# First attention: the softmax of seven of eight head pairs normalised after the product with the values

## The chip, the cores and the metric

The kernel runs on one core of one Trainium2 chip. The metric is the device time of one execution in microseconds (us). A measured time is the median of several runs; the profile comes from one further execution.

## What is computed

Two transformer layers over 512 tokens of 1024 features, in float32, each with adaptive scale and shift, a mixer, and a squared-ReLU MLP. Layer 0 uses a sparse attention with 16 heads (eight pairs), layer 1 a differential attention. The change is in layer 0, whose core is this (`mask` stands for the 128 chosen keys and for the relative bias):

```
def block(args):
    ...
    logits = jnp.einsum('bqhr,bqkr->bhqk', q_lat, kv_sel).astype(jnp.float32)
    bias = rel_bias[_rel_bucket(tpos[None, :, None] - sel)]
    logits = logits + jnp.transpose(bias, (0, 3, 1, 2))
    logits = jnp.where(valid[:, None], logits, NEG)
    p = jax.nn.softmax(logits, axis=-1).astype(h.dtype)
    o_lat = jnp.einsum('bhqk,bqkr->bqhr', p, kv_sel)
    return jnp.einsum('bhqr,hrd->bqhd', o_lat, w_uv)
...
return o.reshape(B, S, A_HEADS * A_V_DIM) @ w_o
```

The softmax divides each row of exponentials by its sum. Whether that division is done on the exponentials or on the product with the values, the result is the same.

## The kernel before, in words

The tokens lie in four tiles of 128 (`i` = 0 to 3), the heads in pairs `p` = 0 to 7 with `m` = 0, 1. One item of the first attention is (p, i, m): a 128-row tile of queries of one head against its 128(i+1) causal keys, so the four tiles are 128, 256, 384 and 512 wide. A function `attend` runs over the 64 items in order. For item n it issues the scores, and for item n - 4 the product with the values:

- `score`: two matmuls into a PSUM bank "l" (L646, L647), a VectorE (DVE) pass that adds mask and bias and finds the row's extreme (L670, L673; the mask with bias comes from GpSimd, L662 and L666), and ScalarE (ACT) exponentials into a tile `ex`, whose row sums go to one of eight columns of the pair's `sums` (L679).
- `pv_a` (the product): reciprocal of the row sum (L943), scaling of the exponentials by it (L944), both on DVE; then `transposed`: TensorE (PE) transposes of the i+1 blocks into a PSUM bank "t" (L687) and a copy to the tile `pt`, by ACT for m = 0 (L690) and by DVE for m = 1 (L692); and, once m = 1 is there, the products of both heads into the pair's bank "o" (L954): head m fills rows 64m to 64m+63, columns are queries.
- `done_a`, after a pair's last item: ACT copies bank "o" to a page `vo` (`bm` for the last pair) (L960), from which the output projection takes its operand (split into a high and a low part by L133 and L134).

PSUM has eight banks, two for each of "d", "l", "t" and "o". While a pair runs, `make_a` prepares the one two ahead: the transposed key weights `uk` (L781) into a "t" bank, keys into a "d" bank (L158 to L160), and copies by DMA. The output projection's steps (L984 to L986) begin inside the last pair and go on behind it; its weights are prepared by ACT (L148) and GpSimd (L153) in pairs 2 to 7. DVE also works off modulation steps at the end of the attention (L433, L435), each on a quarter-megabyte half of a weight row that SP loads into one of three `raw` buffers. What follows the attention begins with the residual's additions (L488).

The order of instructions on each engine is not written out by hand: a scheduler with a model of the chip sets it when the program is built, so an edit in `pv_a` moves its neighbours on all engines. Engines execute their own order strictly and wait for each other by semaphores.

Of the kernel before, what the change touches and what calls it, by code (L numbers as in the profile page):

```python
# [15 lines left out]
ALU = mybir.AluOpType  # L16
# [3 lines left out]
P = 128  # L20
# [3 lines left out]
NT = S // P  # L24
DFF = 4096
HEADS = 16
HD = 64
# [40 lines left out]
def hybrid_kernel(  # L68
# [8 lines left out]
    nc = tc.nc  # L77
    x = x[0]
    out = out[0]
# [11 lines left out]
    def nm(s):  # L91
        uid[0] += 1
        return f"{s}_{uid[0]}"
# [3 lines left out]
    def page(dt=F32, tag="pg"):  # L97
        return pg.tile([P, 512], dt, tag=tag, name=nm(tag), bufs=GB[tag])
# [3 lines left out]
    def temp(tag, dt=F32):  # L102
        return tp.tile([P, 512], dt, tag=tag, name=nm(tag), bufs=TB[tag])

    def small(shape, tag, bufs=4):
        return tp.tile(shape, F32, tag=tag, name=nm(tag), bufs=bufs)
# [3 lines left out]
    def bank(tag):  # L110
        return ps.tile([P, 512], F32, tag=tag, name=nm("ps" + tag), bufs=PB[tag])
# [3 lines left out]
    def wide_bank():  # L115

        tag = ("d", "d", "l", "l", "o", "o")[cyc[0] % 6]
        cyc[0] += 1
        return bank(tag)
# [43 lines left out]
    ident = cp.tile([P, P], F32, name="ident")  # L163
# [137 lines left out]
    for d in range(DC // 2):  # L301
# [10 lines left out]
        for j in range(2):  # L312
            kc = 2 * d + j
            a = (hT[0][:, kc, :], hT[1][:, kc, :])
# [306 lines left out]
    def attend(pairs, make, mask, pv, done, out, LA, early=None, depth=1, group=0, side=iter(()),  # L621
# [18 lines left out]
        def score(it):  # L640
            p, i, m = it
            q, (kh, kl) = qk[p][m]
            W = P * (i + 1)
            h = 2 * p + m
            lp = bank("l")
            nc.tensor.matmul(lp[:, 0:W], q[:, P * i : P * (i + 1)], kl[:, 0:W], start=True, stop=False)  # L646
            nc.tensor.matmul(lp[:, 0:W], q[:, P * i : P * (i + 1)], kh[:, 0:W], start=False, stop=True)  # L647
            neg = temp("neg")
# [6 lines left out]
            near = near[:, ::-1]  # L655
            n0 = max(0, W - 256)
            init = 3e38
            if mask is not None and i >= 3:
                if (i, m) not in full:
                    full[i, m] = page()  # L660
                    nc.gpsimd.tensor_copy(full[i, m][:, 0:n0], mask[i][:, 0:n0])
                marks["p"] = nc.gpsimd.tensor_tensor(out=full[i, m][:, n0:W], in0=mask[i][:, n0:W], in1=near, op=ALU.add).ins  # L662
                near, n0 = full[i, m][:, 0:W], 0
            elif mask is not None and i > 0:
# [74 lines left out]
        for _ in ahead:  # L739
# [7 lines left out]
                            op0=ALU.mult)  # L747
# [55 lines left out]
    for i in range(1, NT):  # L803
        W = P * (i + 1)
        acc = page()
        work[i] = acc
        for h in range(IDXH):
# [4 lines left out]
            r = temp("neg")  # L812
# [4 lines left out]
            else:  # L817
                nc.vector.scalar_tensor_tensor(out=acc[:, 0:W], in0=r[:, 0:W], scalar=s, in1=acc[:, 0:W],
                                               op0=ALU.mult, op1=ALU.add)
# [5 lines left out]
    for i in range(NT):  # L825
        if i % 2 == 0:
            ckb.append(bank("t"))
        o = ckb[-1][:, 256 * (i % 2) : 256 * (i % 2) + 256]
        for k in range(DC):
# [11 lines left out]
    rb = cp.tile([BUCKETS, HEADS], F32, name="rb")  # L841
# [8 lines left out]
                            op0=ALU.subtract)  # L850
# [12 lines left out]
                            op=ALU.mult)  # L863
    lsum = small([1, 4], "lsum", 1)
    nc.vector.tensor_reduce(out=lsum[:, 0:2], in_=lpr.rearrange("o (a d) -> o a d", a=2), axis=mybir.AxisListType.X,
                            op=ALU.add)
# [18 lines left out]
    for i in range(NT):  # L885
        nc.vector.tensor_scalar(out=ckn[i // 2][:, 256 * (i % 2) : 256 * (i % 2) + 256], in0=ck_ps[i],
                                scalar1=ckss[:, i : i + 1], scalar2=None, op0=ALU.mult)
# [17 lines left out]
    for h in range(2):  # L905
        for i in range(NT):
            o = bank("d")
# [28 lines left out]
    a_state = {}  # L936
    oA = {}

    def pv_a(p, i, m, es, sums, transposed):
        W = P * (i + 1)  # L940
        e = es[p, i, m]
        r = small([P, 1], "rs")
        nc.vector.reciprocal(r, sums[:, 2 * i + m : 2 * i + m + 1])  # L943
        nc.vector.tensor_scalar(out=e[:, 0:W], in0=e[:, 0:W], scalar1=r, scalar2=None, op0=ALU.mult)  # L944
        t = transposed(e, i, m == 0)
        a_state[p, i, m] = t
        if i == 0 and m == 0:
            a_state["o", p] = bank("o")
        if m == 1:
            o = a_state["o", p]  # L950
            for j in range(i + 1):
                for mm in range(2):
                    h = 2 * p + mm
                    nc.tensor.matmul(o[64 * mm : 64 * mm + 64, P * i : P * (i + 1)],  # L954
                                     V[j][h // 8][:, 64 * (h % 8) : 64 * (h % 8) + 64],
                                     a_state[p, i, mm][:, P * j : P * (j + 1)], start=(j == 0), stop=(j == i))

    def done_a(p):
        oA[p] = temp("bm") if p == 7 else page(tag="vo")
        nc.scalar.copy(oA[p], a_state["o", p])  # L960

    def mixer_out(w, src, R, ln_idx, prepare, mT, ring, order, late=lambda: None):

# [79 lines left out]
    def scale_residual():  # L1043
        for i in range(NT):
            for h in range(2):
                nc.scalar.activation(R[i][h], R[i][h], AF.Copy, scale=ALPHA)

    attend(range(8), make_a, work, pv_a, done_a, mixer_out(a_w_o[0], oA, R, (0, 0), before_out_a, mT, 6, {(2, 1, 3): "lead", (3, 1, 0): 0, (3, 1, 3): 1}, scale_residual), 4, topk, 2, 2, side)


# [76 lines left out]
    for i in range(NT):  # L1127
        o = wide_bank()
# [6 lines left out]
        t = page()  # L1135
# [129 lines left out]
```

## Time and profile before

| | |
|---|---|
| time, median of 3 runs | 1312.59 us (1311.4 to 1314.78) |
| the profiled execution: its own time | 1311.5 us |
| its span, first to last instruction | 1309.7 us |
| PE busy | 1267.0 us (97%) |
| DVE busy | 741.5 us (57%) |
| ACT busy | 504.2 us (38%) |
| GpSimd busy | 570.5 us (44%) |
| mean granted clock of PE | 0.989 |

How to read it: shares are averages over stages with different limits. The first attention's products run from 172 to 296 us. PE's ends are modelled and its instructions overlap, so a busy PE is not always a PE at its peak; PEld is its weight loads, which overlap the matmuls. The trace names an instruction by its line, engine, operation and tiles (output <- inputs, buffer numbers left out). A helper that records many operations gives them all its own line.

### The profile page before, as it was taken

The numbers are of one execution on the slowest core, as the hardware profiler recorded it, in microseconds if no ns is written. First come the engines' busy times: TensorE is split into PE (matmuls) and PEld (weight loads), VectorE is DVE, ScalarE is ACT, GpSimd is POOL, SyncE is SP. The second block draws the span as 40 slices with busy tenths as digits, with TensorE's granted clock in tenths as the row PEclk, the third lists the DMA queues.
The fourth block names the chain that finished last, engine by engine and source line by source line (L and its number), as shares of the span: only waits on it lengthen the run. The fifth ranks groups of instructions, "written<-read, shape, count | busy, mean of one in ns | idle before, by whom it ended". The sixth has DMA issues, their size and how long they took to land.

```text
span 1309.7 us, 17697 instructions
## 1 busy us (share of the span) xinstructions
PE 1267.0 (97%) x6354; PEld 1013.4 (77%) x6354; DVE 741.5 (57%) x1553; ACT 504.2 (38%) x965; POOL 570.5 (44%) x469
## 2 busy tenths in 40 slices
PE   6999999998999999999999999999899999999997
PEld 4775566677988878878788898877798888888885
DVE  2487859968642774764646376684853342332437
ACT  2554247824432422412315555682453232231320
POOL 1614348604486235234134873451539623424403
PEclk9999999999999999999999999999999999999998
DMA  9727577543623684684422633440144333333311
GB/s 308 215 82 223 168 199 200 150 137 104 187 93 108 201 256 118 210 277 141 141 81 65 177 82 104 129 129 1 49 145 125 100 97 97 97 97 97 97 49 64
DMA packets 169135, 176.79 MB, mean 135 GB/s; under 512 B 13564, under 2 KB 121432, under 8 KB 169048
## 3 DMA queue, kind: packets, MB, share of 16 engines
q1 hardware_dynamic: 169048, 175.67, 45.1%
q8 instruction: 50, 0.82, 0.3%
q14 instruction: 37, 0.30, 0.1%
HBM read 160.93 MB, written 2.12 MB: 124 GB/s over the span
## 4 chain that ended last, share of the span: by engine, by line
PE 72%; DVE 6%; POOL 2%; issue 1%; ACT 1%; DMA 0%; POOLq 0%; DVEq 0%
PE psd L158 5%; PE psd L160 5%; PE psd L159 5%; PE psl L158 3%; PE psl L159 3%; PE psl L160 3%; PE psl L578 3%; PE psl L580 3%; PE psl L579 3%; PE pso L580 3%; PE pso L578 3%; PE psd L580 3%; PE pso L579 3%; PE pso L158 3%; PE psd L578 3%; PE pso L159 3%
## 5 line engine op out<-in xcount | busy, mean ns | idle before, releaser
L153 POOL TENSOR_TENSOR wl<-raw,wh 128x512 fp32r<-128x512 f32 (+1 forms) x226 | 302.2, 1361 | 505.5 <-ACT wh L148 477.7
L148 ACT CAST wh<-raw 128x1024 fp32r<-128x1024 f32 x181 | 189.8, 1050 | 425.0 <-PE psd L580 77.9
L153 DVE TENSOR_TENSOR wl<-raw,wh 128x1024 fp32r<-128x1024 f32 x68 | 91.1, 1339 | 150.0 <-ACT wh L148 150.0
L158 PE MATMUL psd<-htl,wh 128*128 128x512 f32 (+1 forms) x400 | 157.0, 392 | 3.2 <-DVE htl L134 2.7
L159 PE MATMUL psd<-hth,wh 128*128 128x512 f32 (+1 forms) x400 | 155.1, 388 | 0.0
L160 PE MATMUL psd<-hth,wl 128*128 128x512 f32 (+1 forms) x400 | 154.7, 387 | 0.0
L489 POOL TENSOR_TENSOR rq<-rq,pt 128x512 f32<-128x512 f32 x66 | 96.7, 1495 | 76.2 <-DVE pt L488 76.1
L158 PEld LDWEIGHTS psd<-htl,wh 128*128 128x128 f32 x400 | 76.6, 191 | 25.9 <-DVE htl L134 6.0
L679 ACT ACTIVATE ex<-neg,mx 128x128 f32<-128x128 f32 (+3 forms) x128 | 72.1, 564 | 50.3 <-DVE mx L673 42.5
L160 PEld LDWEIGHTS psd<-hth,wl 128*128 128x128 f32 x400 | 76.7, 192 | 16.3 <-issue 1.7
L159 PEld LDWEIGHTS psd<-hth,wh 128*128 128x128 f32 x400 | 76.7, 192 | 13.7 <-issue 0.8
L158 PE MATMUL psl<-htl,wh 128*128 128x512 f32 (+1 forms) x224 | 82.2, 367 | 4.2 <-DVE htl L134 4.2
L159 PE MATMUL psl<-hth,wh 128*128 128x512 f32 (+1 forms) x224 | 81.9, 366 | 0.0
L160 PE MATMUL psl<-hth,wl 128*128 128x512 f32 (+1 forms) x224 | 81.3, 364 | 0.0
L134 DVE TENSOR_TENSOR pg<-ex,pg 128x512 fp32r<-128x512 f32 x66 | 60.4, 917 | 27.1 <-ACT pg L133 27.1
L580 PE MATMUL psl<-wh,pg 128*128 128x512 f32 x176 | 68.9, 391 | 0.0
L578 PE MATMUL pso<-wh,pg 128*128 128x512 f32 x176 | 68.8, 391 | 0.0
L580 PE MATMUL pso<-wh,pg 128*128 128x512 f32 x176 | 68.7, 390 | 0.0
L578 PE MATMUL psl<-wh,pg 128*128 128x512 f32 x176 | 68.7, 390 | 0.0
L579 PE MATMUL pso<-wl,pg 128*128 128x512 f32 x176 | 68.7, 390 | 0.0
L579 PE MATMUL psl<-wl,pg 128*128 128x512 f32 x176 | 68.5, 389 | 0.0
L159 PE MATMUL pso<-hth,wh 128*128 128x512 f32 (+2 forms) x184 | 68.3, 371 | 0.0
(311 smaller groups left out, 2920.9 us busy)
## 6 DMA issues: line engine op xcount, KB each, us to landing
raw<-in_mlp_w_dram SPq DMA_DIRECT2D x128, 512.0 KB, 4.1
raw<-in_ada_w_dram SPq DMA_DIRECT2D x32, 512.0 KB, 4.2
hk<-in_ada_w_dram SPq DMA_DIRECT2D x48, 256.0 KB, 3.6
bm<-in_ada_w_dram SPq DMA_DIRECT2D x48, 256.0 KB, 4.9
raw<-in_b_w_in_dram SPq DMA_DIRECT2D x24, 512.0 KB, 4.0
pg<-pg SPq DMA_DIRECT2D x84, 128.0 KB, 2.4
pg<-in_ada_w_dram SPq DMA_DIRECT2D x32, 256.0 KB, 6.0
raw<-in_a_w_in_dram SPq DMA_DIRECT2D x14, 512.0 KB, 5.1
```

The lines of the kernel that those rows point to most:

```text
L134: eng.tensor_tensor(out=L, in0=src, in1=f(H), op=ALU.subtract)
L148: nc.scalar.copy(Hv, r)
L153: eng.tensor_tensor(out=Lv[:, a:b], in0=r[:, a:b], in1=f(Hv[:, a:b]), op=ALU.subtract)
L158: nc.tensor.matmul(o, w[0], a[1], start=first, stop=False)
L159: nc.tensor.matmul(o, w[0], a[0], start=False, stop=False)
L160: nc.tensor.matmul(o, w[1], a[0], start=False, stop=last)
L489: eng.tensor_tensor(out=R[h], in0=R[h], in1=t, op=ALU.add)
L578: nc.tensor.matmul(o, al[1], wr[0], start=(k == 0), stop=False)
L579: nc.tensor.matmul(o, al[0], wr[1], start=False, stop=False)
L580: nc.tensor.matmul(o, al[0], wr[0], start=False, stop=(k == nk - 1))
L679: marks["a"] = nc.scalar.activation(e[:, 0:W], neg[:, 0:W], AF.Exp, bias=mx[:, 0:1], scale=-1.0, accum_out=sums[:, m : m + 1]).ins
```

## The change

For pairs 0 to 6 the exponentials are no longer scaled: they are transposed as they are, and the transposed copies are all made by DVE. At a pair's last tile (i = 3, m = 0) DVE takes the reciprocal of all eight row sums at once, spreads each over 64 columns of a page, PE transposes that page in four blocks of 128 so that queries become columns, and DVE copies the result back to the page. `done_a` then multiplies the pair's product by that page on DVE, in place of ACT's copy. For pair 7 all stays, its m = 0 copies on ACT too.

```diff
     def pv_a(p, i, m, es, sums, transposed):
-        W = P * (i + 1)
-        e = es[p, i, m]
-        r = small([P, 1], "rs")
-        nc.vector.reciprocal(r, sums[:, 2 * i + m : 2 * i + m + 1])
-        nc.vector.tensor_scalar(out=e[:, 0:W], in0=e[:, 0:W], scalar1=r, scalar2=None, op0=ALU.mult)
-        t = transposed(e, i, m == 0)
+        if p == 7:
+
+            r = small([P, 1], "rs")
+            nc.vector.reciprocal(r, sums[:, 2 * i + m : 2 * i + m + 1])
+            e = es[p, i, m][:, 0 : P * (i + 1)]
+            nc.vector.tensor_scalar(out=e, in0=e, scalar1=r, scalar2=None, op0=ALU.mult)
+        elif i == NT - 1 and m == 0:
+
+            r = small([P, 2 * NT], "rs8", 2)
+            nc.vector.reciprocal(r, sums)
+            a_state["r", p] = page()
+            nc.vector.tensor_copy(a_state["r", p].rearrange("q (a d) -> q a d", d=HD),
+                                  r.unsqueeze(2).to_broadcast([P, 2 * NT, HD]))
+            rb = bank("t")
+            for j in range(NT):
+                c = slice(P * j, P * (j + 1))
+                nc.tensor.transpose(rb[:, c], a_state["r", p][:, c], ident)
+            nc.vector.tensor_copy(a_state["r", p], rb)
+        t = transposed(es[p, i, m], i, p == 7 and m == 0)
         a_state[p, i, m] = t
...
     def done_a(p):
         oA[p] = temp("bm") if p == 7 else page(tag="vo")
-        nc.scalar.copy(oA[p], a_state["o", p])
+        if p == 7:
+            nc.scalar.copy(oA[p], a_state["o", p])
+        else:
+            nc.vector.tensor_tensor(out=oA[p], in0=a_state["o", p], in1=a_state["r", p], op=ALU.mult)
```

In the changed file the reciprocal is L949, the broadcast L951, the added transposes L956, their copy L957, the products with the values L967, the scaling of the product L976, pair 7's reciprocal and scaling L943 and L945, and the output projection L1000 to L1002 (L984 to L986 before).

The scheduler's order changes on all engines within the first attention, and nowhere behind it. Three places follow. On DVE, in the middle of the attention (the end of pair 2), before:

```order
L943 RECIPROCAL rs_2235<-sums_1944 128x1
L944 TENSOR_SCALAR ex_2127<-ex_2127,rs_2235 128x512
L673 ISA neg_2190,mx_2191<-psl_2187,hk_1741 128x128
L673 ISA mx_2191 128x1
L943 RECIPROCAL rs_2259<-sums_1944 128x1
L673 ISA neg_2221,mx_2222<-psl_2218,bm_2223 128x256
L673 ISA mx_2222 128x1
L943 RECIPROCAL rs_2300<-sums_2164 128x1
L944 TENSOR_SCALAR ex_2144<-ex_2144,rs_2259 128x512
L692 COPY pt_2210<-pst_2206 128x384
L944 TENSOR_SCALAR ex_2165<-ex_2165,rs_2300 128x128
```

and of the change (`rs_584` holds eight reciprocals, `pg_2191` is the page they are spread over, `pst_2193` its transposed bank, and the `neg` rows evacuate scores of the next pair):

```order
L949 RECIPROCAL rs_584_2189<-sums_1918 128x8
L673 ISA neg_2175,mx_2176<-psl_2172,bm_2177 128x256
L673 ISA mx_2176 128x1
L692 COPY pt_2112<-pst_2109 128x256
L951 COPY pg_2191<-rs_584_2189 128x512
L692 COPY pt_2142<-pst_2138 128x384
L673 ISA neg_2209,mx_2210<-psl_2206,bm_2211 128x256
L673 ISA mx_2210 128x1
L692 COPY pt_2164<-pst_2160 128x384
L670 ISA neg_2240,mx_2241<-psl_2237,pg_594 128x128
```

The scalings are gone, copies of transposed weights stand in their places, and the broadcast comes three DVE steps behind the reciprocal. On PE at the end of the attention, where pair 7's last tile is transposed and multiplied, before (`pst_3328` is the last transposed tile, `pt_3333` its copy by DVE, and L984 to L986 are steps of the output projection):

```order
L687 MATMUL pst_3328<-ident,ex_3277 128x128 x4
L986 MATMUL psl_3503<-wh_2295,pg_3132 128x512
L984 MATMUL psl_3503<-wh_2393,vo_3174 128x512
L985 MATMUL psl_3503<-wl_2394,pg_3173 128x512
L986 MATMUL psl_3503<-wh_2393,pg_3173 128x512
L984 MATMUL psl_3503<-wh_2515,vo_3219 128x512
L985 MATMUL psl_3503<-wl_2516,pg_3218 128x512
L986 MATMUL psl_3503<-wh_2515,pg_3218 128x512
L984 MATMUL psl_3503<-pg_2613,vo_3250 128x512
L985 MATMUL psl_3503<-pg_2615,pg_3249 128x512
L986 MATMUL psl_3503<-pg_2613,pg_3249 128x512
L954 MATMUL pso_3206<-pt_3323,rq_991 64x128
```

and of the change (`pst_3230` is the last transposed tile, `pt_3235` its copy by DVE, `pt_3225` that of the other head by ACT, `pt_3200` and `pt_3209` belong to the tile before):

```order
L1002 MATMUL psl_3405<-pg_2545,pg_3151 128x512
L687 MATMUL pst_3230<-ident,ex_3179 128x128 x4
L967 MATMUL pso_3108<-pt_3209,rq_991 64x128
L967 MATMUL pso_3108<-pt_3200,rq_1000 64x128
L967 MATMUL pso_3108<-pt_3209,rq_1000 64x128
L967 MATMUL pso_3108<-pt_3200,rq_1009 64x128
L967 MATMUL pso_3108<-pt_3209,rq_1009 64x128
L967 MATMUL pso_3108<-pt_3225,rq_991 64x128
L967 MATMUL pso_3108<-pt_3235,rq_991 64x128
```

Ten steps of the projection stood between the last transposes and the products that need their copy; now five products of the tile before stand there. On DVE ahead of the same copy, before:

```order
L692 COPY pt_3307<-pst_3303 128x384
L435 SCALAR_TENSOR_TENSOR pg_3345<-raw_3371,sil,pg_3345 128x512
L435 SCALAR_TENSOR_TENSOR pg_3346<-raw_3371,sil,pg_3346 128x512
L435 SCALAR_TENSOR_TENSOR pg_3345<-raw_3375,sil,pg_3345 128x512
L435 SCALAR_TENSOR_TENSOR pg_3346<-raw_3375,sil,pg_3346 128x512
L692 COPY pt_3333<-pst_3328 128x512
```

and of the change, from pair 6's product to the first modulation steps and their neighbours:

```order
L976 TENSOR_TENSOR vo_3062<-pso_2846,pg_3012 128x512
L134 TENSOR_TENSOR vo_3076<-vo_2650,pg_3075 128x512
L945 TENSOR_SCALAR ex_3179<-ex_3179,rs_3227 128x512
L433 TENSOR_SCALAR pg_3247<-raw_3249,sil 128x512
L433 TENSOR_SCALAR pg_3248<-raw_3249,sil 128x512
L435 SCALAR_TENSOR_TENSOR pg_3247<-raw_3253,sil,pg_3247 128x512
L435 SCALAR_TENSOR_TENSOR pg_3248<-raw_3253,sil,pg_3248 128x512
L134 TENSOR_TENSOR vo_3152<-vo_3062,pg_3151 128x512
L692 COPY pt_3187<-pst_3184 128x256
```

The sixteen modulation steps (two L433, fourteen L435) now start behind pair 6's product on DVE; before, that product was copied by ACT. The copies of pair 7's last two tiles (384 and 512 wide) still stand among and behind them.

## Rows read from the trace of the kernel before

**Rows 1.** Windows of one pair each: us; busy PE, PEld, DVE, ACT, POOL; PE clock; DMA.

```profile
189.90:202.50 12.60, 12.60 (x92) 8.95 (x89) 11.36 (x45) 10.68 (x29) 9.73 (x12) 1.00 0.63 155
202.50:216.20 13.70, 12.63 (x93) 9.06 (x88) 13.45 (x49) 9.42 (x27) 12.61 (x13) 1.00 0.65 178
216.20:229.40 13.20, 11.39 (x85) 8.16 (x84) 12.48 (x43) 10.89 (x30) 10.49 (x12) 1.00 0.80 224
229.40:240.50 11.10, 10.28 (x83) 7.38 (x81) 8.80 (x34) 9.67 (x28) 8.78 (x10) 1.00 0.83 243
240.50:251.30 10.80, 9.88 (x68) 6.67 (x64) 10.31 (x38) 8.01 (x24) 7.12 (x8) 1.00 0.66 148
```

**Rows 2.** Waits, 200 to 250 us: us in total, times, longest.

```profile
PE psl L646 <- DVE mx L673: 2.5, 4, 1.1
```

**Rows 3.** Groups by line, 200 to 250 us, PEld: busy, mean ns, idle before and releasers.

```profile
L954 PEld LDWEIGHTS pso<-pt,rq 128*64 128x64 f32 x160 | 10.6, 136 | 6.1 <-issue 1.3 <-ACT pt L690 1.2 <-DVE pt L692 1.0
L687 PEld LDWEIGHTS pst<-ident,ex 128*128 128x128 f32 x80 | 9.1, 140 | 5.3 <-issue 4.1 <-PE pso L954 0.2
L646 PEld LDWEIGHTS psl<-pg,pg 128*128 128x128 f32 x32 | 6.2, 194 | 4.4 <-DVE mx L673 2.1 <-issue 1.6 <-DVE rs L943 0.3
...
L781 PEld LDWEIGHTS pst<-ident,uk 128*128 128x128 f32 x6 | 0.6, 140 | 1.1 <-DVE pt L692 1.0 <-issue 0.2
```

**Rows 4.** Groups by line, 200 to 250 us, DVE.

```profile
L944 DVE TENSOR_SCALAR ex<-ex,rs 128x256 f32<-128x256 f32 (+3 forms) x32 | 21.5, 678 | 0.2
L692 DVE COPY pt<-pst 128x512 f32<-128x512 f32 (+3 forms) x16 | 7.6, 475 | 2.2 <-PE pst L687 2.2
...
L943 DVE RECIPROCAL rs<-sums 128x1 f32<-128x1 f32 x31 | 4.8, 153 | 0.0
...
L134 DVE TENSOR_TENSOR pg<-psd,pg 128x512 fp32r<-128x512 f32 x4 | 2.7, 678 | 0.0
```

**Rows 5.** Timeline, 3 to 4 us, DVE: start, us, instruction.

```profile
3.30 0.20 DVE L213 RECIPROCAL sig<-sig 128x8 f32<-128x8 f32 x1
...
3.73 0.29 DVE L216 COPY silrep<-sil 128x256 f32<-128x256 f32 x1
```

**Rows 6.** Timeline: one scaling alone (192.76 us), one beside GpSimd (215.31 us).

```profile
192.76 0.42 DVE L944 TENSOR_SCALAR ex<-ex,rs 128x384 f32<-128x384 f32 x1
...
215.00 1.27 POOL L153 TENSOR_TENSOR wl<-raw,wh 128x512 fp32r<-128x512 f32 x1 [0.41 <-ACT wh L148]
...
215.31 1.17 DVE L944 TENSOR_SCALAR ex<-ex,rs 128x384 f32<-128x384 f32 x1
```

**Rows 7.** Groups by line, 200 to 250 us, ACT.

```profile
L690 ACT COPY pt<-pst 128x128 f32<-128x128 f32 (+3 forms) x16 | 6.7, 419 | 1.4 <-PE pst L687 1.3
...
L960 ACT COPY vo<-pso 128x512 f32<-128x512 f32 x4 | 2.3, 575 | 0.0
```

**Rows 8.** Timeline, 255 to 257 us, PE: eight transposes, then scores.

```profile
255.47 1.16 PE L479 MATMUL pst<-ident,g 128*128 128x128 f32 x8
256.38 0.31 PE L646 MATMUL psl<-pg,pg 128*128 128x128 f32 x1
```

**Rows 9.** Timeline, 274 to 297 us, DVE and PE: the attention's end.

```profile
274.79 1.19 DVE L433 TENSOR_SCALAR pg<-raw,sil 128x512 f32<-128x512 f32 x2
...
285.10 1.41 DVE L435 SCALAR_TENSOR_TENSOR pg<-raw,sil,pg 128x512 f32<-128x512 f32 x2 [1.16 <-DMA raw<-in_ada_w_dram]
...
287.06 2.92 DVE L435 SCALAR_TENSOR_TENSOR pg<-raw,sil,pg 128x512 f32<-128x512 f32 x4
292.72 0.69 DVE L692 COPY pt<-pst 128x512 f32<-128x512 f32 x1 [2.74 <-PE pst L687]
...
294.13 0.39 PE L984 MATMUL psl<-pg,vo 128*128 128x512 f32 x1
...
294.58 0.39 PE L986 MATMUL psl<-pg,pg 128*128 128x512 f32 x1
...
294.90 1.09 PE L954 MATMUL pso<-pt,rq 128*64 128x128 f32 x16
```

## The prediction, made before the changed kernel ran

> **What bounds the kernel now.** The change touches the first attention alone, so I read its stretch: the busy time by windows (each window is about the period of one pair of heads), then the groups by line for VectorE (DVE), ScalarE (ACT) and TensorE's weight loads (PEld) in 200 to 250 us, then the timeline where two engines meet. [rows 1] show two regimes. From 189.9 to 202.5 us TensorE (PE) is busy for all 12.60 us. In the next two periods DVE is busy 13.45 of 13.70 and 12.48 of 13.20 us, and PE falls to 12.63 and 11.39: DVE sets the pace. In the fourth DVE has air (8.80 of 11.10) and the period is the shortest of those that still build a pair's keys. Over the five, PE idles 61.4 - 56.78 = 4.6 us; its largest named wait is for the scores' evacuation on DVE [rows 2]. The true gap is larger, since an idle load is hidden under the modelled end of the matmul before it. In [rows 3] the four load groups of the attention idle 6.1 + 5.3 + 4.4 + 1.1 = 16.9 us, of which 1.3 + 4.1 + 1.6 + 0.2 = 7.2 waited for nothing shown (runs of one kind after another): 9.7 us waited for other engines. So 4.6 to 9.7 us of PE are to be had, no more. After 256 us PE runs attention and output projection back to back, and ahead of 190 us it has the mixer's other products as filler.
>
> **What the change does to each engine, per pair (pairs 0 to 6).**
> DVE loses 8 scalings and 8 reciprocals: 8 x 0.678 + 8 x 0.153 = 6.6 us [rows 4]. It gains four weight copies, 4 x 0.475 = 1.9 us [rows 4]; one reciprocal of 128x8, 0.20 us [rows 5]; a broadcast copy of 128x512; and two full-width passes over PSUM (the transposed reciprocals, and the product, which reads PSUM and one page like L134), 2 x 0.678 = 1.36 us [rows 4]. No row has a broadcast of 512; one of 256 took 0.29 us [rows 5], and a scaling of 128x384 took 0.42 us alone and 1.17 us beside a GpSimd subtraction that began 0.3 us before it [rows 6]. So the broadcast lies between 0.29 and 1.17 us; I take 0.7, as half of these run beside GpSimd. Sum 4.2 us: DVE sheds 2.4 us per pair, and 12.5 to 13.4 us become 10 to 11.
>
> The Trainium skill (SBUF — State Buffer, Who interferes with whom) says that VectorE's two-port copies and scalings lock GpSimd's port pair, and that an instruction with one SBUF input outside those modes does not. [rows 6] agree; by it the broadcast alone of the added work can stall, and in all seven pairs the sum for DVE would be 7 x (1.17 - 0.7) = 3.3 us worse.
>
> ACT loses four copies and the output's copy, 4 x 0.419 + 0.575 = 2.25 us per pair [rows 7]. It is not the bound (9 to 11 us of 11 to 14 in [rows 1]), but the loads waited 1.2 us for its copies [rows 3].
>
> A copy of a weight tile costs DVE 0.475 us where ACT took 0.419 [rows 4, 7]: 28 x 0.056 = 1.6 us if every one lay on PE's path. The Trainium skill (Perfetto Trace Analysis, Optimizing Scalar/DVE Operations) speaks against this half of the change: it advises moving work from a saturated VectorE to ScalarE, and it gives a PSUM access as about 125 ns for VectorE and 51 for ScalarE. By that the forecast would be an estimated 28 x 0.074 = 2.1 us later; no run here shows the two figures apart.
>
> PE gains four 128x128 transposes per pair. Eight back to back took 256.38 - 255.47 = 0.91 us [rows 8], so 0.114 each: 28 x 0.114 = **+3.2 us**, on the path wherever PE binds, and nothing covers them once the gaps are gone. The runs of products and of transposes change little, so I add nothing for switching.
>
> New waits. (a) The added transposes wait in PE's order for the reciprocal and its broadcast, and the copy of their result must free a bank of the two "t" banks. At best 0; at worst, with PE having nothing ahead, 0.20 + 1.17 + 0.68 = 2.1 us per pair. The order shown above puts one or more other DVE steps between reciprocal and broadcast, and PE has scores and products there, so I take 0.1: **+0.7 us** in all. (b) The tail. Before, after the last pair's last four transposes PE had ten projection products, and their DVE copy finished under these (292.72 to 293.41, the products to 294.90) [rows 9]. Now thirteen rows of products follow the last transposes at once, five of them for the tile before, so most of that copy is bare: 0 to 0.69 us plus what DVE is late. DVE comes to it through the sixteen modulation steps L433 and L435, whose loads set their pace: from 274.79 us to 287.06 + 2.92 = 289.98 us, 15.2 us, with a wait of 1.16 us for a load [rows 9]. Before, DVE then had 2.74 us to spare; now those steps start behind pair 6's product on DVE, and pair 6's last weights come behind twelve projection products, 12 x 0.225 = 2.7 us (two products start within 0.45 us in [rows 9]). The spare time is used up. I take **+0.8 us**, between 0 and 3.
>
> The moved rows on SP are a few loads of keys, bias strips and residuals, and the spare three "raw" buffers still gate the modulation loads; I cost them at nothing, since SP waits for buffers, and DVE's tail above carries what remains of it. GpSimd's order keeps its work; it is spared seven of eight scalings that could lock it out. Behind the attention no row changes its place, so the rest of the span moves as a block.
>
> **Sum.** Of the gaps I recover 6 us: all that PE's own rows show (4.6) and about a quarter of the rest, as loads that idle for 0.2 to 0.4 us partly lie under a matmul and DVE stays four fifths busy. -6.0 + 3.2 + 0.7 + 0.8 = **-1.3 us**. The profiled execution took 1311.5 us, 1.1 below the median of 1312.59; from the median the forecast is **1311.3 us**. What a measurement of this kernel tells from no change is about 0.3%, 3.9 us, so I expect no difference that can be told.
>
> **Rivals.**
> *Faster: DVE was the only brake.* All 9.7 us come back and the new waits hide: -9.7 + 3.2 + 0.3 = -6.2, 1306.4 us. For it: the period of 11.1 us with DVE at 8.80 [rows 1], and a shorter way from exponential to transpose, since no scaling stands between. Against it: the window in which PE was busy 12.60 of 12.60 us, and the 3.2 us that PE has to add. Chance 0.26.
> *Slower: the lock step.* Reciprocal, broadcast, four transposes, copy, with PE and DVE waiting for each other in turn and two banks for ten users per pair where there were nine, all but one freed by DVE where ACT freed half. At 1.2 us per pair: -6.0 + 3.2 + 8.4 + 0.8 = +6.4, 1319.0 us. It decides from (6.0 - 3.2 - 0.8 + 3.9) / 7 = 0.84 us per pair. For it: the bound of 2.1, and PE's in-order queue. Against it: in the order the reciprocal is early. Chance 0.19, which also takes in the tail (b) at its worst.
> *It does not do what it says*: DVE stays the brake since the broadcast and two passes each meet GpSimd. With the broadcast at 1.17 us DVE still sheds 6.6 - 4.7 = 1.9 us per pair, so this stays inside the forecast.
>
> **How the numbers follow.** Forecast 0.55, faster 0.26, slower 0.19; with the tail (b) at 0 or at 3 us the first lies between -2.1 and +0.9 us, well within 3.9, so these are also the chances of same, faster and slower. The range reaches from a little under the faster case, 1305.5, to 1317.0, where the lock step costs 0.9 us per pair; less than 2 in 10 lie outside, mostly above.
>
> **What would show it.** Right: in 200 to 250 us DVE busy 40 us or less, PE's waits for DVE's scores nearly gone, L956 behind few and short waits, the end of the attention (the first L488) 1 to 2 us earlier than 299.75, and the windows behind it unchanged. A new idle row of several tenths of a us ahead of L956, or of the products behind the last transposes, shows the slower cases; periods under 11.5 us from 200 us on show the faster one. The forecast is wrong if the time behind the attention changes, or if PE's gaps in 200 to 250 us stay near 4.6 us.

## The result, and the profile after

The changed kernel took **1328.61 us** (median of 4 runs, 1324.4 to 1329.71) against 1312.56 us for the kernel before on the same chip: ratio 1.0114, 95% interval 1.0097 to 1.0132. By the ratio it is slower by 15 us, and the forecast of 1311.3 us, with its range up to 1317.0, is wrong.

The page of the changed kernel: span and busy time. PE is busy 10 us longer than the 1267.0 of before, at a larger span; VectorE and ScalarE are busy less.

```profile
span 1327.6 us, 17705 instructions
...
PE 1276.8 (96%) x6382; PEld 1019.6 (77%) x6382; DVE 739.6 (56%) x1497; ACT 491.7 (37%) x930; POOL 565.7 (43%) x469
```

Where the time went is a matter of place first. The end of the attention, the first L488, before and after (timeline, VectorE: start, us, instruction):

```profile
299.75 1.37 DVE L488 TENSOR_TENSOR pt<-psd,hk 128x512 f32<-128x512 f32 x2 [1.69 <-PE psd L986]
```

```profile
317.41 1.37 DVE L488 TENSOR_TENSOR pt<-psd,hk 128x512 f32<-128x512 f32 x2 [1.73 <-PE psd L1002]
```

It comes 17.66 us later, and the whole span grew by 1327.6 - 1309.7 = 17.9 us. The first exponentials start at 156.10 and 156.59 us, so 17.2 us of this are lost inside the first attention; behind it the rest moved as a block.

The windows of the changed kernel (us; busy PE, PEld, DVE, ACT, POOL; PE clock; DMA), to be held against [rows 1]: first the sum over 200 to 250 us, then the first stall in steps of 3 us, then 170 to 300 us.

```profile
200.00:250.00 50.00, 46.72 (x318) 33.41 (x314) 35.87 (x118) 27.06 (x72) 36.09 (x38) 0.93 0.60 161
...
187.00:190.00 3.00, 1.97 (x12) 1.16 (x9) 2.56 (x13) 0.83 (x4) 1.43 (x2) 1.00 0.85 215
190.00:193.00 3.00, 1.09 (x2) 0.40 (x2) 0.52 (x4) 0.55 (x2) 0.73 (x1) 0.63 0.47 127
193.00:196.00 3.00, 1.83 (x6) 1.57 (x7) 1.13 (x5) 0.67 (x2) 0.85 (x1) 0.50 0.80 177
196.00:199.00 3.00, 2.92 (x14) 1.96 (x13) 2.49 (x5) 1.65 (x5) 0.33 (x1) 0.73 0.44 98
...
170.00:300.00 130.00, 119.02 (x738) 84.01 (x737) 85.41 (x270) 59.77 (x159) 62.53 (x69) 0.95 0.49 134
```

The same stretch of 130 us before:

```profile
170.00:300.00 130.00, 124.64 (x809) 89.56 (x808) 99.32 (x332) 75.03 (x198) 65.45 (x69) 1.00 0.62 170
```

VectorE did fall, as forecast: 35.87 us of 50, and 13.9 us less in 170 to 300. But PE stands idle for 130 - 119.02 = 11.0 us where it had 5.4 before, and its granted clock, 1.00 in every window of [rows 1], fell to 0.50 (1.2 instead of 2.4 GHz) in 193 to 196 us, after PE had been busy for 1.09 us of the three before. Over the 130 us the clock is 0.95. If work at half the clock takes twice as long (the four added transposes L956 took 1.05 us there, the same four 0.66 us at 1.00 in own_pin below), that alone is an estimated 119.02 x 0.05 = 6.0 us.

The timeline shows what began it (start, us, instruction, idle time before it and what ended that):

```profile
181.37 2.13 SPq L128 DMA_DIRECT2D raw<-in_a_w_o_dram  x2
183.55 0.47 SPq L353 DMA_DIRECT2D pg<-ex  x1
184.12 0.63 SPq L354 DMA_DIRECT2D pg<-ex  x1
...
192.45 0.51 ACT L679 ACTIVATE ex<-neg,mx 128x256 f32<-128x256 f32 x1 [3.53 <-DMA pg<-ex]
...
193.09 0.29 DVE L670 CUSTOM_DVE_ANT_0 neg<-psl,pg 128x128 f32<-128x128 f32 x1 [2.54 <-ACT ex L679]
...
193.94 0.42 DVE L951 COPY pg<-rs 128x512 f32<-128x512 f32 x1
...
194.17 0.76 PE L646 MATMUL psl<-pg,pg 128*128 128x512 f32 x1 [2.38 <-DVE mx L673]
...
195.16 1.05 PE L956 MATMUL pst<-ident,pg 128*128 128x128 f32 x4
...
196.25 0.69 DVE L957 COPY pg<-pst 128x512 f32<-128x512 f32 x1 [1.89 <-PE pst L956]
...
226.02 0.61 ACT L679 ACTIVATE ex<-neg,mx 128x384 f32<-128x384 f32 x1 [3.88 <-DMA pg<-ex]
...
227.52 0.33 PE L646 MATMUL psl<-pg,pg 128*128 128x128 f32 x1 [2.28 <-DVE mx L673]
```

Read it from the DMAs down. L353 and L354 are two small copies that build the query stack of a later pair (in `qstacks`) out of a temporary `ex`; they are issued behind the 512-KB loads of the output weights. An exponential, which also writes an `ex`, waits 3.53 us until they have landed. VectorE waits for the exponential (the two `neg` buffers are full), PE for VectorE's score evacuation. The new chain lies in the same knot: the broadcast L951 stands behind the waiting evacuations on VectorE, the transposes L956 behind the waiting scores on PE, and run at the lower clock. The same happens again at 222 to 228 us; there the clock is 0.56 and 0.50 in the two 3-us windows from 228 on.

ScalarE's waits in 180 to 300 us (us in total, times, longest), after and then before:

```profile
ACT ex L679 <- PE pst L687: 24.6, 15, 2.7
...
ACT ex L679 <- DMA pg<-ex: 7.4, 2, 3.9
```

```profile
ACT ex L679 <- DMA pg<-ex: 1.2, 1, 1.2
...
ACT ex L679 <- PE pst L687: 1.2, 2, 0.6
```

Both waits are new in size. The exponentials share six `ex` buffers with the query stacks' temporary L. Those DMAs were as slow before the change (first line, 8.1 us from issue to landing) as after it (second line, 7.3):

```profile
pg<-ex SPq DMA_DIRECT2D x2, 128.0 KB, 8.1
```

```profile
pg<-ex SPq DMA_DIRECT2D x2, 128.0 KB, 7.3
```

What moved is who inherits their buffer. In the compiled order of ScalarE, the exponential of pair 1 that must wait for a DMA queue is the third block's second head before, and two items earlier after:

```
before  126 L679 ACTIVATE ex_1889,sums_1738<-neg_1883,mx_1884 128x384 [waits DMAHW2_49,DMAHW1_49,DVE_49]
after   117 L679 ACTIVATE ex_1828,sums_1726<-neg_1823,mx_1824 128x256 [waits DMAHW1_49,DMAHW2_49,DVE_49,Pool_49]
```

No edit of the diff touches `ex` or the DMAs. The scheduler hands out buffers in the order in which it thinks they come free. The chain (reciprocal, broadcast, four transposes and copy back), written ahead of a pair's last transposes, keeps two of the six occupied for longer: this is how I read the two orders, and the runs below test it.

### The profile page after: what moved, and what is told of

Its sections match the earlier page's. It is cut to its first block, busy times and chain, and to the rows that moved or that the text cites. A ratio compares the mean times of both kernels' runs of the same rounds, so it can differ in the third digit from the quotient of the medians.

```text
span 1327.6 us, 17705 instructions
## 1 busy us (share of the span) xinstructions
PE 1276.8 (96%) x6382; PEld 1019.6 (77%) x6382; DVE 739.6 (56%) x1497; ACT 491.7 (37%) x930; POOL 565.7 (43%) x469
## 4 chain that ended last, share of the span: by engine, by line
PE 79%; DVE 7%; DMA 7%; POOL 2%; ACT 2%; issue 2%; SPq 1%; POOLq 0%; DVEq 0%; ACTq 0%
PE psd L158 6%; PE psd L160 6%; PE psd L159 6%; PE psl L158 3%; PE psl L159 3%; PE psl L160 3%; PE psl L578 3%; PE psl L580 3%; PE psl L579 3%; PE pso L158 3%; PE pso L579 3%; PE pso L580 3%; PE pso L578 3%; PE psd L580 3%; PE psd L578 3%; PE psd L579 3%
## 5 line engine op out<-in xcount | busy, mean ns | idle before, releaser
L679 ACT ACTIVATE ex<-neg,mx 128x128 f32<-128x128 f32 (+3 forms) x128 | 71.8, 562 | 80.5 <-DVE mx L673 40.0
L134 DVE TENSOR_TENSOR pg<-ex,pg 128x512 fp32r<-128x512 f32 x66 | 60.7, 921 | 26.2 <-ACT pg L133 26.2
```

The costliest lines, as they stand in the source:

```text
L134: eng.tensor_tensor(out=L, in0=src, in1=f(H), op=ALU.subtract)
L679: marks["a"] = nc.scalar.activation(e[:, 0:W], neg[:, 0:W], AF.Exp, bias=mx[:, 0:1], scale=-1.0, accum_out=sums[:, m : m + 1]).ins
```

## The experiments

The ratios below are against the kernel before, run beside each kernel on the same chip; 0.1% is 1.3 us.

**Is it the shared buffer?** The stack's temporary gets a buffer of its own, in the changed kernel and, as a control, in the one before (the reciprocal's buffer goes from two to one to make room):

```
-    TB = {"neg": 2, "ex": 6, "pt": 4, "bm": 3, "hk": 3}
+    TB = {"neg": 2, "ex": 6, "el": 1, "pt": 4, "bm": 3, "hk": 3}
-        A, C, L = page(F32R), page(F32R), temp("ex", F32R)
+        A, C, L = page(F32R), page(F32R), temp("el", F32R)
```

> The changed kernel; only the low halves of a pair's query stack (written by GpSimd, read by two small DMAs) get a buffer of their own instead of one of the six that the exponentials rotate through. Theory 1 (held buffer): in the changed kernel the exponential that inherits the stack's buffer stands two items earlier in the first pairs, the two small DMAs land only 7 to 8 us after their issue behind 512-KB loads, ScalarE waits 3.5 us at 189 and 3.9 us at 222, PE follows it into two gaps and then runs at half the clock. Then both waits go, the granted clock is 1.00 from 190 to 240, and the kernel takes 1315 to 1319 us. Theory 2 (lock step of reciprocal, broadcast, transposes and copy): the step is untouched, so 1326 to 1331. Theory 3 (the copies that moved to DVE): also 1326 to 1331.

> The same edit on the kernel before, as a control. Theory 1: there only one exponential waits on such a DMA, 1.2 us, and PE does not follow, so 1310 to 1314. If a buffer more is worth something by itself, 1305 to 1309, and the gain of the other run has to be read against this one.

Measured: own_after 1317.01 us, ratio **1.0055** (1.0036 to 1.0073); own_before 1313.46 us, 1.0002 (0.9984 to 1.0019). The buffer takes back half of the loss, 0.59% or 7.7 us, and is worth nothing to the kernel before. The wait on the DMAs is gone from ScalarE's list, the stretch at 190 us has its clock again, but the other new wait is as long as it was:

```profile
187.00:190.00 3.00, 2.48 (x21) 1.62 (x21) 2.98 (x7) 2.12 (x6) 2.00 (x2) 1.00 0.74 184
190.00:193.00 3.00, 3.00 (x27) 2.05 (x23) 2.59 (x13) 2.01 (x5) 0.87 (x2) 1.00 0.75 170
193.00:196.00 3.00, 3.00 (x23) 2.08 (x22) 2.49 (x9) 1.75 (x7) 3.00 (x3) 1.00 0.51 125
```

```profile
ACT ex L679 <- PE pst L687: 24.7, 19, 2.8
```

Theory 1 (the held buffer) is right for half of the loss, and does not reach the other half.

**Is it the copies?** One run puts the first head's copies back on ScalarE in the changed kernel, one moves them to VectorE in the kernel before:

```
-        t = transposed(es[p, i, m], i, p == 7 and m == 0)
+        t = transposed(es[p, i, m], i, m == 0)
...
-        t = transposed(e, i, m == 0)
+        t = transposed(e, i, p == 7 and m == 0)
```

> The changed kernel with one part undone: the first head's transposed weights of all pairs are copied by ScalarE as before; the normalisation on the product stays. Theory 1: the exponential that inherits the stack's buffer stands as early as in the change (pair 1, second block, second head), so the stall stays and it takes 1324 to 1331. Theory 3 (DVE copies): back to 1310 to 1316. Theory 2 (lock step): 1322 to 1331.

> The kernel before with the other part alone: weights normalised ahead of their transposes as before, the copies of pairs 0 to 6 by DVE. Theory 1: the exponential that inherits the buffer stands one item earlier than before in pairs 1, 3 and 4, so little stall; DVE gains 28 copies (0.28 to 0.69 us each, 13.6 us in 100) that it has no room for: 1314 to 1322. Theory 3: 1322 or more. Theory 2: 1310 to 1314.

Measured: act_copy 1333.98 us, 1.0165 (1.0125 to 1.0205), above what any of the theories had and, with intervals that barely overlap, slower than the change; dve_copy 1316.89 us, 1.0045 (1.0029 to 1.0061). The copies alone cost the kernel before some 6 us, where VectorE had no room [rows 1]. Putting them back does not help the changed kernel: its stall stays, and ScalarE waits 11.8 us on the stack's DMAs there, in 160 to 320 us, where the change has 7.4.

**Is it ScalarE's wait for the residual?** own_after still had a gap of PE at 236 us, with ScalarE ahead of it waiting for x's transfers (timeline and window of own_after):

```profile
235.59 0.63 ACT L1062 ACTIVATE rq<-rq 128x512 f32<-128x512 f32 x1 [3.01 <-DMA rq<-in_x_dram]
```

```profile
240.00:250.00 10.00, 9.22 (x57) 6.25 (x57) 7.32 (x25) 6.51 (x19) 5.90 (x7) 0.83 0.69 174
```

So the scalings were to be placed later, again with a control, and two other kernels ran on that base: one without the chain, one with the copies on ScalarE.

```
+                with tc.issue_after(a_state["m", 6]):
                     nc.scalar.activation(R[i][h], R[i][h], AF.Copy, scale=ALPHA)
...
-            (reciprocal, broadcast, four transposes, copy back)
+            a_state["r", p] = hT[0][:, 0, :]
```

> The changed kernel with the stack's own buffer (as in own_after) and a second edit: ScalarE's eight scalings of the residual x (L1062 of the change) may not be placed ahead of the last product of pair 6. In own_after the first four stand in pair 4, ScalarE waits 3.0 and 1.6 us there for x's transfers, behind it stand the exponentials and a 2.4-us wait of DVE, PE has a gap of 2.05 us at 236 and runs at a granted clock of 0.83 in 240 to 250. Theory 1, widened (the relieved ScalarE queue runs into transfers that have not landed): this second wait goes too, and the kernel takes 1308 to 1313 us, level with the kernel before. Theory 2 (lock step): 1315 to 1318, since the x wait would be hidden.

> Both edits on the kernel before, as a control. Its own scalings wait 0.8 us each, three times, and PE does not follow: 1309 to 1313 by every theory.

> As own_late, but pairs 0 to 6 leave out the reciprocals, their broadcast, the four transposes and the copy back; the product is multiplied by a page of other data, so its time stands for the change with no chain at all. The 28 transposes alone are 3.2 us of PE and the seven copies and broadcasts 7.8 us of DVE. Theory 2 (lock step): 6 us or more below own_late. Theory 1: 3 to 4 us below it, the transposes' own PE time and no more.

> As own_late, with the first head's transposed weights of all pairs copied by ScalarE again. Theory 1: without the two kinds of stall it does not matter much who copies: within 3 us of own_late. Theory 3 (DVE's copies cost the time): 3 us or more below own_late.

Measured: own_late 1318.48 us, 1.0041 (1.0025 to 1.0057); control 1315.64 us, 1.0015 (1.0 to 1.003); **no_chain 1306.18 us, 0.9955** (0.9939 to 0.9970); own_late_act 1320.27 us, 1.0052 (1.0034 to 1.0069). As a test of the wait for x, own_late is void: the edit tied the scalings to an operation of VectorE and they stayed in pair 4, with a wait of 2.20 us. The other two speak. Without the chain the kernel is 0.86% or 11 us faster than with it, not the 3 to 4 us that theory 1 had; this is the size of theory 2 (the lock step), not yet its mechanism. And who copies the weights makes no difference that these intervals tell once the buffer is free.

**Root or second cause?** If the chain is what holds the buffers, the shared buffer should not matter without it, and moving the chain behind the pair's last products should free them. The first two kernels keep the shared buffer, the others have the stack's own:

```
 chain_out:       the chain left out, other data in its place
 chain_late(_own):
-        elif i == NT - 1 and m == 0:        (ahead of transposed(...))
+        if p < 7 and i == NT - 1 and m == 1:  (behind the products)
 chain_no_pe:
-            rb = bank("t") ... transposes ... tensor_copy(a_state["r", p], rb)
+            nc.vector.tensor_copy(a_state["r", p], f(hT[0][:, 0, :]))
```

> The changed kernel with one thing left out: the reciprocals, their broadcast, transposes and copy back of pairs 0 to 6; the product is multiplied by a page of other data. The stack's buffer stays shared. Theory 4 (the chain is the root of both losses: standing ahead of the pair's last transposes, it holds two of the six weight buffers, so the next pair's exponentials wait for those transposes and fall onto the stack's buffer two to three items early): without the chain the inheriting exponential stands at pair 1's fourth block, later than in the kernel before, no wait on the stack's transfers, granted clock 1.00 throughout, 1304 to 1309 us. If the held buffer were a loss beside the chain, as theory 1 had it: 1314 to 1319.

> The changed kernel with the chain moved behind the pair's last products (written after the last item's matmuls instead of ahead of the last block's transposes); same work, the stack's buffer stays shared. Theory 4: the last transposes no longer wait, the inheriting exponential goes back to where it stood before in pairs 1, 3 and 4, and what is left is the transposes' own 3.2 us of PE: 1308 to 1314 us. Theory 2 in its narrow form (the chain's own waits between reciprocal, copy, transposes and copy, wherever they stand): 1316 or more.

> As chain_late, with the stack's own buffer. Theory 4: the same time as chain_late within 3 us, 1307 to 1313, since the early need of the buffer is gone already. Theory 1: 4 us or more below chain_late.

> The changed kernel with the stack's own buffer; of the chain the reciprocal, the broadcast and a copy of equal size from other data stay on VectorE where they are, the four transposes and their bank are left out, so that nothing of PE stands behind the broadcast. Theory 4: the last transposes need not wait, so 1304 to 1310, within 3 us of the run without a chain. If VectorE's added 7.8 us were the cost: 1312 to 1317.

Measured: chain_out 1306.4 us, **0.9971** (0.9957 to 0.9985); chain_late 1320.87 us, 1.0073 (1.0045 to 1.0101); chain_late_own 1319.19 us, 1.0050 (1.0024 to 1.0076); chain_no_pe 1312.05 us, 1.0009 (0.9990 to 1.0029). Half of theory 4 (the chain is the root of both losses) holds: without the chain the inheriting exponential is pair 1's fourth block, ScalarE waits for none of the stack's DMAs, and the shared buffer costs next to nothing (0.9971 with it, 0.9955 without, intervals that overlap). So the held buffer is a consequence of the chain and not a second fault. With the shared buffer, moving the chain behind the products also takes 1.0114 to 1.0073. The other half falls: with the stack's own buffer the chain is about as dear behind the products (1.0050) as ahead of them (1.0055), and chain_no_pe, which theory 4 had within 3 us of no chain, is 5 us above chain_out. The place is not the rest of the price; the chain's work, or its links, are.

**Which part of the chain?** The scalings are now tied to ScalarE's own last exponential of pair 6, and stay there:

```
+            last_exp[p] = marks["a"]
...
+                with tc.issue_after(last_exp[6]):
```

> The changed kernel with the stack's own buffer, and ScalarE's scalings of the residual x now placed behind the last exponential of pair 6 (the earlier try tied them to an operation of VectorE, and they stayed in pair 4, where ScalarE waited up to 2.2 to 3.0 us for x). Theory 1, widened (the relieved ScalarE queue runs into transfers): the wait for x, PE's gap near 236 to 242 and the lower clock behind it (0.83 in 240 to 250) go, and the ratio to the kernel before falls from 1.0055 to 1.000 to 1.003. If that gap has another cause (the order around the chain): 1.004 to 1.006 as before.

> The same two edits, and of the chain only VectorE's part is left (reciprocal, broadcast, a copy of equal size from other data; no transposes, no bank). Without the second edit it had a gap in the same place, with a wait of 3.3 us for x on ScalarE, and 1.0009. Theory 1, widened: the gap goes, 0.995 to 0.998, as without any chain, so VectorE's added 7.8 us cost nothing by themselves. If VectorE's time counts: 1.000 to 1.002.

> Both edits, and the chain written behind the pair's last products. If the place of the chain ahead of the last transposes costs something: 2 us or more below own_pin. If only its work counts: level with own_pin within 2 us.

> As own_pin, with the chain's two copies (broadcast and copy back, 0.42 to 0.93 and 0.69 us on VectorE) made by ScalarE, which has more room. If VectorE's order holds the chain up (the broadcast stands behind score evacuations, the copy back ahead of the last weights' copies): 2 to 4 us below own_pin, 0.997 to 1.001. If the links PE to copy to PE are what costs, whoever copies: level with own_pin, or slower, a ScalarE copy of 512 columns being 0.57 us and more.

> Both edits (the stack's own buffer, the scalings placed late); of the chain only PE's part is left: the four transposes of a page that is ready long before, into their bank, in the same place; reciprocal, broadcast and copy back are left out, and the product is multiplied by other data. The complement of no_pe_pin (1.0007), between no chain (0.9955) and the whole (1.0050). If PE's own 3.2 us is all that its part costs: 0.997 to 0.999. If the bank costs as much again, though nothing reads it: 1.000 to 1.003.

> As no_pe_pin, but the broadcast and the copy write 128x64 instead of 128x512, and the page is free again at once; reciprocal, number of operations and place stay. If VectorE's time in the chain (7.8 us in no_pe_pin, some 3 us here) is the price: 0.996 to 0.999. If it is the place in VectorE's order: 1.000 to 1.002 as no_pe_pin.

| kernel (own buffer in all, scalings tied as above in all but no_chain) | what of the chain is left | us | ratio (interval) |
|---|---|---|---|
| no_chain | nothing | 1306.18 | 0.9955 (0.9939 to 0.9970) |
| small_dve | VectorE's part, 128x64 wide | 1306.97 | 0.9972 (0.9958 to 0.9986) |
| pe_only | transposes and bank | 1309.1 | 0.9993 (0.9977 to 1.0010) |
| no_pe_pin | VectorE's part, 128x512 wide | 1312.63 | 1.0007 (0.9989 to 1.0025) |
| act_chain | all, its copies on ScalarE | 1316.78 | 1.0036 (1.0019 to 1.0053) |
| own_pin | all | 1319.34 | 1.0050 (1.0030 to 1.0069) |
| late_own_pin | all, behind the products | 1321.41 | 1.0076 (1.0063 to 1.0089) |

By the ratios the scalings were not it: own_pin, where they no longer wait before the first L488, has 1.0050, own_after 1.0055. The parts of the chain nearly add up instead. Against no chain, VectorE's part costs 1.0007 - 0.9955 = 0.52%, 6.8 us; PE's part 0.38%, 5.0 us; together 11.8, and the whole chain 0.95%, 12.5 us. By the intervals each of these differences is good to some 0.25% (3 us), and they compare kernels run on different chips; on no_chain's own chip, against own_late, the whole is 0.86%. The same VectorE operations an eighth as wide cost 0.17%. That is no clean test of VectorE's time: small_dve also frees its page at once, and in the traces its broadcasts and copies take 5.8 us against 9.2 in no_pe_pin, 3.4 us less, where the ratios differ by 0.35%, 4.6 us. On ScalarE the chain's copies are no dearer, perhaps cheaper (the intervals overlap).

A second measure comes from the traces: the time from the first exponential to the first L488, which leaves out that these executions enter the attention some 5 us apart. Each trace is one execution: those of no_chain, pe_only and own_pin are the fastest of their runs, those of small_dve and no_pe_pin the slowest.

| kernel | first exponential | first L488 | between, us |
|---|---|---|---|
| small_dve | 156.12 | 295.68 | 139.56 |
| no_chain | 151.93 | 291.70 | 139.77 |
| chain_out | 156.25 | 296.39 | 140.14 |
| pe_only | 151.72 | 294.64 | 142.92 |
| before | 156.10 | 299.75 | 143.65 |
| no_pe_pin | 157.03 | 301.85 | 144.82 |
| own_pin | 151.81 | 300.38 | 148.57 |
| late_own_pin | 156.46 | 307.81 | 151.35 |
| own_late_act | 156.44 | 308.21 | 151.77 |
| own_after | 151.88 | 305.06 | 153.18 |
| the change | 156.59 | 317.41 | 160.82 |

By it the transposes and their bank cost 142.92 - 139.77 = 3.15 us, which is PE's own time in the forecast; VectorE's part 5.05; together 8.20, and the whole chain in own_pin 8.80. Neither half has the chain's links between PE and VectorE, so 0.7 us by the ratios (give or take some 4.6) and 0.60 by the traces are left for the lock step, which the prediction had at 8.4. PE's own waits for the chain in own_pin come to 1.9 us (180 to 300 us):

```profile
PE pst L690 <- DVE pg L960: 1.1, 3, 0.4
...
PE pst L959 <- DVE pg L954: 0.8, 2, 0.5
```

own_after lies 4.61 us above own_pin here, so whether the wait for x costs something stays open.

How can work on a VectorE that is busy only seven tenths of the time cost so much? Here are ScalarE's waits in 180 to 300 us and PE's busy time in 170 to 300 us. First no_chain, then small_dve, no_pe_pin, pe_only and own_pin, in which L681 and L690 are the L679 and L687 of the change:

```profile
ACT ex L679 <- DVE mx L673: 21.9, 17, 2.2
...
ACT ex L679 <- PE pst L687: 2.4, 3, 1.4
...
170.00:300.00 130.00, 129.33 (x824) 94.57 (x823) 92.11 (x278) 62.41 (x164) 63.27 (x69) 1.00 0.58 163
```

```profile
ACT ex L681 <- PE pst L690: 7.0, 6, 1.9
```

```profile
ACT ex L681 <- PE pst L690: 10.0, 9, 3.5
...
170.00:300.00 130.00, 125.76 (x803) 90.45 (x802) 92.48 (x286) 61.63 (x162) 63.45 (x69) 0.99 0.62 168
```

```profile
ACT ex L681 <- PE pst L690: 13.0, 11, 2.8
...
170.00:300.00 130.00, 128.62 (x837) 95.14 (x833) 87.10 (x270) 62.71 (x164) 60.40 (x65) 1.00 0.58 162
```

```profile
ACT ex L681 <- PE pst L690: 23.8, 18, 2.8
...
ACT ex L681 <- DVE mx L675: 3.3, 3, 1.7
```

With the chain the exponentials wait for the transposes that free their `ex`: 2.4 us with no chain, 23.8 with the whole. It is tempting to read a loop from this, in which whatever stands ahead of a pair's last transposes delays the release of the weight buffers and with them the next pair. But three observations speak against taking these waits for the price. The exponentials' wait for VectorE's evacuations falls from 21.9 to 3.3 us at the same time; the two together are 24.3 and 27.1 us. In own_late_act, where ScalarE also makes copies and these wait in their stead, their wait for the transposes is short, and the kernel is as slow as own_late:

```profile
ACT ex L679 <- PE pst L687: 3.2, 1, 3.2
```

And where half of the 23.8 us is spent, PE has no gap. In 190 to 230 us, no_chain first, then own_pin, where 12.8 us of that wait fall:

```profile
190.00:230.00 40.00, 40.00 (x292) 29.23 (x291) 30.73 (x111) 28.56 (x77) 35.81 (x39) 1.00 0.77 207
```

```profile
190.00:230.00 40.00, 40.00 (x293) 29.05 (x290) 33.55 (x115) 25.91 (x70) 31.91 (x35) 1.00 0.68 185
...
ACT ex L681 <- PE pst L690: 12.8, 8, 2.8
```

PE is busy throughout at the full clock, with as many matmuls (293 and 292), so those waits open no gap there. own_pin loses PE time at the ends of the attention: it is busy 17.95 of 20 us in 170 to 190, around the first pair's chain, and 37.80 of 40 in 230 to 270, where no_chain has 20.00 and 40.00. VectorE's part shows the same. Up to 250 us small_dve and no_pe_pin do alike (PE busy 59.56 and 59.59 of 60 from 190 on); then, in this order:

```profile
250.00:270.00 20.00, 19.71 (x115) 15.00 (x116) 13.01 (x46) 9.99 (x28) 4.27 (x4) 1.00 0.05 14
```

```profile
250.00:270.00 20.00, 17.21 (x89) 13.20 (x88) 10.05 (x31) 8.91 (x22) 4.59 (x5) 0.91 0.13 42
```

One wait of PE for VectorE's L134 (2.79 us, at 253.21 us) and the lower clock behind it make most of the difference between these two traces. So the price is shown by leaving parts out; how VectorE's part comes to cost its 5 to 7 us is not. What the traces show, beside PE's own added work, is a few gaps of PE at the ends of the attention, not an even toll on every pair. A seventh `ex` buffer, which would test the loop, was not tried. No version here that keeps the whole normalisation beat the kernel before.

## Why the prediction was wrong

- **"Of the gaps I recover 6 us": right in kind, and near in size.** chain_out, which is the change without its chain, gains 0.29%, 3.8 us; no_chain, with the stack's own buffer besides, 0.45%, 5.9 us, and its trace leaves PE 130 - 129.33 = 0.7 us idle of the 5.4 before. VectorE was a brake, and taking the scalings away does release it. (The upper bound of 9.7 us was read somewhat high: for 2.3 of it the trace's list of waits names no other engine.)
- **"+0.7" for the chain's waits: the step that failed first.** The "+3.2" for PE's transposes fits pe_only (3.15 us by its trace, 5.0 give or take 3 by the ratios). The waits I priced at 0.1 us per pair, since "the order shown above puts one or more other DVE steps between reciprocal and broadcast", and VectorE's work in the chain at nothing, since I netted it against the scalings. With the buffer free the whole chain costs 12.5 us by the ratios (8.8 by own_pin's trace); its VectorE part alone, with no link to PE at all, costs 6.8 (5.05 by the trace). Why it does stays open.
- **The lock-step rival came out at the right number by luck.** It gave 1319.0 us, and the change with the stack's own buffer has 1.0050 to 1.0055, about 1319.5. But its mechanism, PE and VectorE waiting for each other, is not where most of the cost lies: the two halves without any link already cost 11.8 of the 12.5 us, and PE's waits for the chain are 1.9 us where the rival had 8.4.
- **"The moved rows on SP ... I cost them at nothing": the step that failed second.** Not SP's rows but the ring of `ex` moved: the chain changed which exponential inherits the buffer that a small DMA still reads. I looked at who executes what in which order, not at which earlier user each buffer comes from. The wait on the stack's DMAs went from 1.2 to 7.4 us in 180 to 300 us, and with the clock it is worth 7.7 us.
- **The clock** stood at 1.00 in [rows 1] and in every term. In the changed kernel two gaps of PE are each followed by some microseconds at 0.50; an estimated 6 us of the trace's 17.7 are that.
- **Right:** VectorE busy 35.87 us of 50 (forecast 40 or less); "the rest of the span moves as a block"; the broadcast at 0.7 us (L951 was 0.42 at 193.94 us, and 1.25 us beside a GpSimd subtraction, mean 0.67 over seven). By the port rule of the Trainium skill (SBUF — State Buffer, Who interferes with whom) a copy like this can be locked out by GpSimd; the 1.25 us agree, and the seven broadcasts together stayed at the price.
- **The copies:** moving them to VectorE alone costs the kernel before 0.45%, 5.9 us. That agrees in direction with the Trainium skill's advice that moving work from a saturated VectorE to ScalarE may pay (Perfetto Trace Analysis, Optimizing Scalar/DVE Operations); the 2.1 us estimated from that section's figures is too little here. In the changed kernel, where VectorE is no longer saturated, moving them back gains nothing. The tail (0.8) was not separated.

The sum by the runs: -5.9 for the gaps, +12.5 for the chain, +7.7 for the held buffer: +14.3 us of the 15 measured. This sum is no test, since each term is the difference of two neighbouring kernels and they must add up to the change; only the halves of the chain (11.8 against 12.5) could have come out otherwise.

The Trainium skill's hint that the same gap repeated for a stretch on the engine that should be saturated can mean too few buffers for the next tile (Perfetto Trace Analysis, Optimization Strategy) is not borne out here: the repeated wait was ScalarE's, while PE, the engine that should be saturated, was busy 40.00 of 40 us.

## What to carry to other kernels

Before costing a moved or added step by its engine time alone, list the buffers that stay occupied because of it, and who takes each of them next. Here a buffer whose earlier user was a small DMA behind large loads meant two waits of 3.5 and 3.9 us that no edit in the diff names, and a buffer of its own for that temporary gave back half of the loss. A busy share of 70% is no proof of room: VectorE's added work cost 5 to 7 us, which only runs with parts left out could tell. And a long total of waits is not yet a cause: look at whether the engine that is nearly always busy lost time in that stretch, and for a run that is as slow without the wait.

## What was not expected of the hardware

A gap of PE can be dearer than its length. In the changed kernel PE was busy 1.09 us in 190 to 193, and in the next 6 us its clock was granted at 0.50 and 0.73 although there was work; with the stack's temporary in a buffer of its own the clock stayed at 1.00 in all three windows. Not every gap does this: in own_pin PE was busy 1.84 of the 3 us from 184 on, and the clock stayed at 1.00. And narrowing a VectorE operation saved less than its width: the broadcast and the copy took 0.37 and 0.46 us each 64 columns wide, 0.59 and 0.73 us 512 wide (means of seven each, small_dve and no_pe_pin).
